# Down pieces taken in two parts between single gate and up pieces, and down weights laid two rows to a partition

## The chip, the core and the metric

The kernel runs on one core of a Trainium2 chip. The metric is device time in microseconds from start to end of one execution. Engines: PE (TensorE) multiplies matrices and loads their stationary operands (PEld in the profile); DVE (VectorE), ACT (ScalarE) and POOL (GpSimd) work on elements; SP (SyncE) issues transfers. Sixteen DMA engines move data between HBM and the on-chip memory SBUF; PE writes its results to PSUM.

## The reference

One encoder block on 528 tokens of width 1024: a mixer (attention beside a convolution), then a mixture of 16 experts in which every expert picks its 66 tokens. The part that this change touches is the experts':

```python
def one_group(hs):
    logits = jnp.einsum('ld,de->le', hs, w_router)
    aff = jax.nn.softmax(logits, axis=-1)
    g, idx = lax.top_k(aff.T, cap)                      # cap = 66
    xg = hs[idx]
    a = jnp.einsum('ecd,edf->ecf', xg, w_gate)          # d 1024, f 2048
    u = jnp.einsum('ecd,edf->ecf', xg, w_up)
    y = jnp.einsum('ecf,efd->ecd', jax.nn.silu(a) * u, w_down)
    y = y * g[..., None]
    out = jnp.zeros((L, D), y.dtype).at[idx.reshape(-1)].add(y.reshape(-1, D))
```

All weights are fp32, 24 MB for an expert.

## The kernel before

The mixer and the routing fill the first 355 us. Then a loop runs over the experts `e`. The weights come in pieces of 1 MB, 8 KB to each of 128 partitions, into a ring of 20 tiles called `raw`. A list `tasks`, written out by hand, sets the order of the pieces; `pump` issues a transfer for each free tile of the ring, in that order, and `nextw` hands PE the next piece and pumps again. A tile is free when PE has done its last matmul on it. SP issues nearly all transfers, so a transfer whose tile isn't free holds up those behind it.

An expert has 16 gate and up pieces (256 rows of the weights by 1024 columns, so two rows to a partition, row `p` and row `128 + p` of the piece) and 8 down pieces (256 rows by 1024 columns, laid out in the same way, two runs of 4 KB in a partition). In the loop over expert `e` PE works on gate and up pieces of expert `e` and on down pieces of expert `e - 1`.

- `prod` multiplies gate or up weights: the weights are the stationary operand, in halves of 64 columns, and the 66 chosen tokens `X` move past. Results go to PSUM as `G` or `U`, then through ACT (SiLU) and DVE (product) to `H`, in which partition `p` of slice `j` holds hidden unit `128 j + p`. A piece is 32 matmuls in the program; the chip runs each as two pairs of weight load and matmul, so a piece is 64 pairs in the trace.
- `down_piece` multiplies with down weights: 32 columns of `H` are the stationary operand and 512 columns of the weights move past. Four such matmuls run side by side on four column groups of PE (a set). A piece has three rounds `r` of four matmuls, which the chip runs as six sets, 24 pairs. Results add up in the PSUM tile `y`, three banks, which has one buffer.
- `to_tokens` scatters what an earlier expert gave (`yh`, `yl`) to the tokens by a matmul with a one-hot matrix: tile `T`, two matmuls; DVE adds it to `acc`.
- `down_rows`, at an expert's end, reads `y` with ACT and DVE (lines 980 to 987) and leaves `yh` and `yl`.

The order on PE is that of the program. With `i` counting the gate and up pieces of an expert, a token product and a whole down piece stand behind every odd `i`, so the pattern is two gate or up pieces, `T`, one down piece. I call it a group; there are eight in an expert. Expert 0 has gate and up pieces alone; the last expert's down pieces follow the loop, cut into 512 rows by 512 columns.

Of the kernel before, what the change touches and what calls it, by code (L numbers as in the profile page):

```python
# [19 lines left out]
P = 128  # L20
D = 1024
DC = D // P
# [32 lines left out]
def block_kernel(ctx: ExitStack, tc: tile.TileContext, x, meta, mix_g, w_in, conv_w, lq1, lk1, lq2,  # L55
                 lk2, sub_g, w_out, ffn_g, w_router, w_gate, w_up, w_down, fin_g, rope, out):
    nc = tc.nc
# [18 lines left out]
    def two(ap):  # L76
# [28 lines left out]
    rows = [(meta, NMETA, 0), (x[0, 0:128], 128, 16), (x[0, 128:256], 128, 144), (x[0, 256:384], 128, 272),  # L105
            (x[0, 384:496], 112, 400), (x[0, 496:512], NMETA, 512)]
# [121 lines left out]
    HS = (slice(0, HALF), slice(HALF, L))  # L228
# [353 lines left out]
    last = [Outs(0, c, None) for c in range(0, D, 256)]  # L582
# [132 lines left out]
    def moe_raw():  # L715
        i = moe_n[0] % NRAW
        moe_n[0] += 1
        for n, p in rings:
            if i < n:
                return p.tile([P, 2048], F32, name="raw", tag="raw")  # L720
            i -= n

    tasks = []
    def gate_up(e):
        return [w[0, e, k * 256:(k + 1) * 256, h * 1024:(h + 1) * 1024].rearrange("(c p) f -> p c f", p=P)
                for h in range(2) for w in (w_gate, w_up) for k in range(4)]

    def down(e):

        for d in range(8):  # L730
            rows, cols = slice(d * 256, (d + 1) * 256), slice(0, D)
            if e == NE - 1:
                rows, cols = slice(d % 4 * 512, (d % 4 + 1) * 512), slice(d // 4 * 512, (d // 4 + 1) * 512)
            yield w_down[0, e, rows, cols].rearrange("(c p) f -> p c f", p=P)


    for e in range(NE):
        dn = down(e - 1) if e else None
        for i, t in enumerate(gate_up(e)):
            tasks.append(t)  # L740
            if e and i % 2:
                tasks.append(next(dn))
    tasks.extend(down(NE - 1))
    queue = []

    def pump(n, eng=nc.sync):
        while len(queue) < n and tasks:
            t = moe_raw()
            a = tasks.pop(0)
            v = t.rearrange("p (c f) -> p c f", c=a.shape[1])  # L750
            if tasks:
                eng.dma_start(v, a)
            else:
                for k in range(2):
                    eng.dma_start(v[:, 2 * k:2 * k + 2], a[:, 2 * k:2 * k + 2])
            queue.append(t)

    pump(RING[0])


# [77 lines left out]
    nc.vector.tensor_tensor(af, af, r2[:, :, None].to_broadcast([P, NT, NE]), op=ALU.mult)  # L838
    nc.scalar.activation(af, af, AF.Exp)
    pump(NRAW - RING[3])  # L840
    late.close()

# [55 lines left out]
    def gather(e):  # L898
        xg = xgp.tile([CAP, D], F32, name="xg", tag="xg")
        nc.gpsimd.indirect_dma_start(out=xg, out_offset=None, in_=hn2_d,  # L900
                                     in_offset=bass.IndirectOffsetOnAxis(ap=idxT[:CAP, e:e + 1], axis=0))
        return xg
# [7 lines left out]
    last = const.tile([P, 2], F32, name="last")  # L910
# [16 lines left out]
    HS = [wk.tile([P, NF, CAP], F32, name=f"H{i}") for i in range(2)]  # L927
# [3 lines left out]
    def banks(tag, n):  # L931
        return ps2.tile([P, n, 512], F32, name=tag, tag=tag, bufs=1)

    def nextw():
        pump(NRAW)
        return queue.pop(0)

    def prod(out, w, c0, x, first, last):

        for q in range(2):  # L940
            nc.tensor.matmul(out[64 * q:64 * q + 64], w[:, c0 + 64 * q:c0 + 64 * q + 64], x, start=first, stop=last,  # L941
                             skip_group_check=True)

    def at(t, i):
        return t[:, i // 4, i % 4 * CAP:(i % 4 + 1) * CAP]

    def four(t, k):
        return t[:, k, :4 * CAP].rearrange("p (c n) -> p c n", n=CAP)

    def turn_x(X, xg, k):  # L950
        t = banks("T", 1)
        for i in range(4):
            nc.tensor.transpose(at(t, i), xg[:, (4 * k + i) * P:(4 * k + i + 1) * P], ident[:CAP, :CAP])  # L953
        nc.vector.tensor_tensor(X[:, 4 * k:4 * k + 4], four(t, 0),
                                gffn[:, 4 * k:4 * k + 4, None].to_broadcast([P, 4, CAP]), op=ALU.mult)

    def new_x():
        return wk.tile([P, DC, CAP], F32, name="X", tag="X", bufs=2)

    def down_piece(y, H, d):  # L960


        w = nextw()
        for r in range(3):
            ob, ci = ((0, 0), (0, 1), (1, 0))[r]
            o = ci * 1024 + ob * 512
            for g in range(3):
                nc.tensor.matmul(y[32 * g:32 * g + 32, ob], H[:, 2 * d + ci, GR[g]:GR[g] + 32], w[:, o:o + 512],  # L968
                                 start=d == 0 and r != 1, stop=d == 7 and r != 0, skip_group_check=True)
            nc.tensor.matmul(y[96:128, r], H[:, 2 * d + 1, GR[r]:GR[r] + 32], w[:, 1536:2048], start=d == 0, stop=d == 7,  # L970
                             skip_group_check=True)

    def down_rows(y, e):

        gate = at96[:96, NE + e:NE + e + 1]
        yh = wk.tile([96, D], FR, name="yh", tag="yh")
        yl = wk.tile([96, D], FR, name="yl", tag="yl")
        tmp = wk.tile([96, 512], F32, name="tmp", tag="tmp")
        a, b = slice(0, 512), slice(512, D)
        nc.scalar.activation(yh[:, a], y[:96, 0], AF.Copy, scale=gate)  # L980
        nc.vector.scalar_tensor_tensor(yl[:, a], y[:96, 0], gate, f32(yh[:, a]), op0=ALU.mult, op1=ALU.subtract)
        for g in range(3):
            gs = slice(32 * g, 32 * g + 32)
            nc.scalar.activation(tmp[gs], y[96:128, g], AF.Copy, scale=at96[gs, NE + e:NE + e + 1])
        nc.vector.scalar_tensor_tensor(tmp, y[:96, 1], gate, tmp, op0=ALU.mult, op1=ALU.add)
        nc.scalar.copy(yh[:, b], tmp)
        nc.vector.tensor_tensor(yl[:, b], tmp, f32(yh[:, b]), op=ALU.subtract)  # L987
        oh = wk.tile([96, 512], FR, name="oh", tag="oh")
        nc.gpsimd.tensor_scalar(oh, tok, at96[:96, e:e + 1], None, op0=ALU.is_equal)  # L989
        return oh, yh, yl  # L990

    def to_tokens(po, rows, d):

        oh, yh, yl = rows
        hf, t = divmod(d, 4)
        hfs = slice(hf * 512, (hf + 1) * 512)
        for n, b in enumerate((yh, yl)):
            nc.tensor.matmul(po, oh[:, t * P:(t + 1) * P], b[:, hfs], start=n == 0, stop=n == 1)  # L998
        nc.vector.tensor_tensor(acc[:, t, hfs], acc[:, t, hfs], po, op=ALU.add)  # L999
# [3 lines left out]
    X = new_x()  # L1003
# [3 lines left out]
    rows = None  # L1007
    for e in range(NE):
        H = HS[e % 2]
        y = banks("y", 3) if e else None  # L1010
        i = 0
        for h in range(2):
            for n in range(2):
                t = banks("GU"[n], 2)
                for k in range(4):
                    w = nextw()
                    for ci in range(2):
                        c = 2 * k + ci
                        for j in range(8):
                            prod(at(t, j), w, ci * 1024 + j * P, X[:, c], c == 0 and j % 4 == 0, c == DC - 1)  # L1020
                    if i % 2 and rows is not None:
                        to_tokens(banks("T", 1)[:, 0], rows, i // 2)
                    if i % 2 and e:
                        down_piece(y, HS[(e - 1) % 2], i // 2)
                    i += 1
                    if i in (10, 12) and e + 1 < NE:
                        if i == 10:
                            Xn = new_x()
                        turn_x(Xn, xg, i // 2 - 5)
                        if i == 12 and e + 2 < NE:  # L1030
                            xg = gather(e + 2)
                for k in range(2):
                    dst = H[:, 8 * h + 4 * k:8 * h + 4 * k + 4]
                    src = four(t, k)
                    if n == 0:
                        nc.scalar.activation(dst, src, AF.Silu)  # L1036
                    else:
                        nc.vector.tensor_tensor(dst, dst, src, op=ALU.mult)  # L1038
        if e:
            rows = down_rows(y, e - 1)  # L1040
        X = Xn
# [25 lines left out]
    for k in range(2):  # L1067
        t = moe_raw()
        o += [t[:, :D], t[:, D:]]
    t = moe_raw()  # L1070
# [7 lines left out]
    for i in range(8):  # L1078
        w = nextw()
        hf, d = divmod(i, 4)  # L1080
        for ci in range(4):
            f = 4 * d + ci
# [81 lines left out]
```

## Time and profile before

| what | value |
|---|---|
| runs | 1375.6, 1375.21 and 1371.81 us, median 1375.21 |
| profiled execution | 1375.47 us, of which the span from first to last instruction is 1373.7 us |
| PE busy | 1258.4 us, 92% of the span |
| weight loads busy (beside PE) | 929.4 us, 68% |
| DVE, ACT, POOL busy | 390.3, 232.0, 175.6 us |
| moved by DMA | 434.49 MB |
| mean granted TensorE clock | 0.968 |

An engine's busy share says how much of the span it had an instruction under way, and PE's matmuls overlap, so a busy PE isn't one at its peak. A share near 100% for two units at once doesn't tell which one sets the time. That is told by waits: who stood idle, and what ended it.

### The profile page before, as it was taken

The page shows a single profiled execution, that of the slowest core. Times are in us where ns is not written, and L with a number is a line of the kernel's source. Part 1 is how long each engine was busy: PE and PEld are TensorE (multiplying, and loading weights), DVE is VectorE, ACT ScalarE, POOL GpSimd, SP SyncE. Part 2 cuts the span into 40 slices and gives each one's busy share as a digit, 9 for nine tenths or more (in the row PEclk, how much of TensorE's full clock was granted, in tenths as well). Part 3 has the DMA queues.
Part 4 walks back from the last instruction along what each step waited for, and adds up shares of the span by engine and source line. Part 5 has one row for each costly group of instructions (what it writes and reads, how often), then busy time and mean ns, then how long its engine had stood idle before and what let it go on. Part 6 is the DMA issues. An engine that isn't in the chain of part 4 may idle for free.

```text
span 1373.7 us, 47053 instructions
## 1 busy us (share of the span) xinstructions
PE 1258.4 (92%) x22308; PEld 929.4 (68%) x22308; DVE 390.3 (28%) x668; ACT 232.0 (17%) x431; POOL 175.6 (13%) x139
## 2 busy tenths in 40 slices
PE   7888889995579999999999999999999999999996
PEld 6678889995566666666666666666666666665665
DVE  5876776554100111121111111111111111111114
ACT  4455444332000101010010101011010101010112
POOL 2734441231100000000000000000000000000002
PEclk9899889997799999999999999999999999999998
DMA  7311211295799999999999999999999999999994
GB/s 208 93 31 31 62 32 62 93 355 199 285 358 403 396 401 401 390 407 395 407 397 405 386 394 395 392 398 390 400 383 400 394 387 397 390 398 398 407 367 166
DMA packets 142881, 434.49 MB, mean 316 GB/s; under 512 B 13200, under 2 KB 37776, under 8 KB 142688
## 3 DMA queue, kind: packets, MB, share of 16 engines
q1 hardware_dynamic: 139936, 423.49, 80.6%
q0 software_dynamic: 2752, 8.00, 1.9%
q8 instruction: 174, 2.85, 0.9%
q14 instruction: 19, 0.16, 0.0%
HBM read 427.19 MB, written 4.26 MB: 314 GB/s over the span
## 4 chain that ended last, share of the span: by engine, by line
PE 76%; DMA 8%; DVE 7%; issue 4%; ACT 3%; POOL 1%; SPq 0%; DVEq 0%; ACTq 0%; POOLq 0%
PE y L968 21%; PE G L941 17%; PE U L941 17%; PE T L998 5%; PE pj L274 5%; DMA raw<-in_w_gate 4%; PE pj L304 3%; DMA raw<-in_w_up 3%; PE ys L941 1%; ACT qsw L365 1%; PE sc L430 1%; PE pj L344 1%; PE T L953 1%; ACT p L441 1%; DVE wl L234 1%
## 5 line engine op out<-in xcount | busy, mean ns | idle before, releaser
L968 PE MATMUL y<-raw,H 128*32 128x512 f32 x2160 | 336.9, 596 | 2.1 <-issue 2.1
L970 PE MATMUL y<-raw,H 128*32 128x512 f32 x720 | 331.9, 596 | 0.0
L941 PEld LDWEIGHTS U<-X,raw 128*64 128x64 f32 x8192 | 250.5, 138 | 65.1 <-issue 49.3
L941 PEld LDWEIGHTS G<-X,raw 128*64 128x64 f32 x8192 | 249.9, 139 | 59.7 <-issue 52.5
L941 PE MATMUL U<-X,raw 128*64 128x66 f32 x8192 | 262.9, 224 | 21.5 <-issue 16.7
L941 PE MATMUL G<-X,raw 128*64 128x66 f32 x8192 | 261.7, 224 | 19.3 <-issue 18.0
L999 DVE TENSOR_TENSOR acc<-acc,T 128x512 f32<-128x512 f32 x112 | 76.9, 687 | 600.0 <-PE T L998 600.0
L968 PEld LDWEIGHTS y<-raw,H 128*32 128x32 f32 x2160 | 79.8, 109 | 190.2 <-issue 175.2
L1036 ACT ACTIVATE H<-G 128x264 f32<-128x264 f32 x64 | 21.5, 388 | 592.0 <-PE G L941 592.0
L900 POOL DMA_INDIRECT xg<-hn_rows,idxT x16 | 16.3, 1017 | 694.8 <-PE T L953 675.2
L274 PE MATMUL pj<-xh,wl 128*128 128x264 f32 x320 | 70.0, 302 | 0.0
L970 PEld LDWEIGHTS y<-raw,H 128*32 128x32 f32 x720 | 69.1, 109 | 0.9 <-issue 0.6
L274 PE MATMUL pj<-xl,wh 128*128 128x264 f32 x320 | 68.6, 298 | 0.0
L274 PE MATMUL pj<-xh,wh 128*128 128x264 f32 x320 | 68.3, 297 | 0.0
L980 ACT ACTIVATE yh<-y,at 96x512 fp32r<-96x512 f32 x15 | 10.3, 684 | 282.2 <-PE y L970 282.2
L998 PE MATMUL T<-yh,oh 96*128 96x512 f32 x112 | 55.9, 499 | 1.6 <-issue 1.6
L274 PEld LDWEIGHTS pj<-xh,wl 128*128 128x128 f32 x320 | 53.9, 204 | 0.1
L274 PEld LDWEIGHTS pj<-xl,wh 128*128 128x128 f32 x320 | 53.3, 202 | 0.0
L274 PEld LDWEIGHTS pj<-xh,wh 128*128 128x128 f32 x320 | 53.3, 202 | 0.0
L989 POOL TENSOR_SCALAR oh<-tok,at 96x512 fp32r<-96x512 int16 x15 | 23.6, 1573 | 174.8 <-PE T L998 174.7
L998 PE MATMUL T<-yl,oh 96*128 96x512 f32 x112 | 44.4, 396 | 1.6 <-DVE yl L987 1.6
L1038 DVE TENSOR_TENSOR H<-H,U 128x264 f32<-128x264 f32 x64 | 24.4, 423 | 70.9 <-PE U L941 70.9
(225 smaller groups left out, 1181.5 us busy)
## 6 DMA issues: line engine op xcount, KB each, us to landing
raw<-in_w_up SPq DMA_DIRECT2D x128, 1024.0 KB, 11.1
raw<-in_w_gate SPq DMA_DIRECT2D x126, 1024.0 KB, 21.2
raw<-in_w_down SPq DMA_DIRECT2D x126, 1024.0 KB, 20.4
raw<-in_w_in SPq DMA_DIRECT2D x24, 512.0 KB, 4.2
raw<-in_w_out SPq DMA_DIRECT2D x8, 512.0 KB, 3.5
hn_rows<-raw SPq DMA_DIRECT2D x4, 512.0 KB
raw<-in_w_gate POOLq DMA_DIRECT2D x2, 1024.0 KB, 9.5
out<-raw SPq DMA_DIRECT2D x4, 512.0 KB, 4.6
```

The costliest lines, as they stand in the source:

```text
L234: nc.vector.tensor_tensor(lo, src, f32(hi), op=ALU.subtract)
L274: nc.tensor.matmul(o[:, hf * 512:hf * 512 + HALF], a[:, c], b[:, HS[hf]], start=c == 0 and n == 0, stop=c == DC - 1 and n == 2)
L304: nc.tensor.matmul(o[:, hf * 512:hf * 512 + HALF], a[:, k, i * P:(i + 1) * P], b[:, HS[hf]], start=k == 0 and n == 0, stop=k == 3 and n == 2)
L900: nc.gpsimd.indirect_dma_start(out=xg, out_offset=None, in_=hn2_d, in_offset=bass.IndirectOffsetOnAxis(ap=idxT[:CAP, e:e + 1], axis=0))
L941: nc.tensor.matmul(out[64 * q:64 * q + 64], w[:, c0 + 64 * q:c0 + 64 * q + 64], x, start=first, stop=last, skip_group_check=True)
L968: nc.tensor.matmul(y[32 * g:32 * g + 32, ob], H[:, 2 * d + ci, GR[g]:GR[g] + 32], w[:, o:o + 512], start=d == 0 and r != 1, stop=d == 7 an ...
L970: nc.tensor.matmul(y[96:128, r], H[:, 2 * d + 1, GR[r]:GR[r] + 32], w[:, 1536:2048], start=d == 0, stop=d == 7, skip_group_check=True)
L989: nc.gpsimd.tensor_scalar(oh, tok, at96[:96, e:e + 1], None, op0=ALU.is_equal)
L998: nc.tensor.matmul(po, oh[:, t * P:(t + 1) * P], b[:, hfs], start=n == 0, stop=n == 1)
L999: nc.vector.tensor_tensor(acc[:, t, hfs], acc[:, t, hfs], po, op=ALU.add)
L1036: nc.scalar.activation(dst, src, AF.Silu)
L1038: nc.vector.tensor_tensor(dst, dst, src, op=ALU.mult)
```

## The change

Three things change together. The order of the tasks: a down piece stands behind every gate or up piece with even `i` instead of odd, so a group's pieces come as gate, down, gate. The work on it: `down_piece` takes the piece and the rounds to run; round 0 runs behind even `i`, rounds 1 and 2 behind odd `i`, with the token product ahead of them. The layout: a down piece now puts rows `2p` and `2p + 1` of its 256 rows in partition `p`, so that a partition's 8 KB are one run in HBM. For this, `H` must hold its hidden units in the same order, and gate and up weights are read at every second column (`step=2`). The last expert's down pieces take rows in the same order; their runs stay 2 KB long.

```diff
             if e == NE - 1:
                 rows, cols = slice(d % 4 * 512, (d % 4 + 1) * 512), slice(d // 4 * 512, (d // 4 + 1) * 512)
-            yield w_down[0, e, rows, cols].rearrange("(c p) f -> p c f", p=P)
+                yield w_down[0, e, rows, cols].rearrange("(b p c) f -> p b c f", p=P, c=2)
+            else:
+                yield w_down[0, e, rows, cols].rearrange("(p c) f -> p c f", p=P)
...
-            if e and i % 2:
+            if e and i % 2 == 0:
                 tasks.append(next(dn))
...
-    def prod(out, w, c0, x, first, last):
+    def prod(out, w, c0, x, first, last, step=1):
 
         for q in range(2):
-            nc.tensor.matmul(out[64 * q:64 * q + 64], w[:, c0 + 64 * q:c0 + 64 * q + 64], x, start=first, stop=last,
+            c = c0 + 64 * q * step
+            nc.tensor.matmul(out[64 * q:64 * q + 64], w[:, c:c + 63 * step + 1:step], x, start=first, stop=last,
                              skip_group_check=True)
...
-    def down_piece(y, H, d):
-
-
-        w = nextw()
-        for r in range(3):
+    def down_piece(y, H, d, w, rounds):
+
+
+        for r in rounds:
...
-                            prod(at(t, j), w, ci * 1024 + j * P, X[:, c], c == 0 and j % 4 == 0, c == DC - 1)
+                            prod(at(t, j), w, ci * 1024 + j // 2 * 256 + j % 2, X[:, c], c == 0 and j % 4 == 0,
+                                 c == DC - 1, 2)
                     if i % 2 and rows is not None:
                         to_tokens(banks("T", 1)[:, 0], rows, i // 2)
-                    if i % 2 and e:
-                        down_piece(y, HS[(e - 1) % 2], i // 2)
+                    if e:
+                        if i % 2 == 0:
+                            wd = nextw()
+                        down_piece(y, HS[(e - 1) % 2], i // 2, wd, ((0,), (1, 2))[i % 2])
```

On PE, where one expert ends and the next begins, with the semaphores that an instruction waits for in brackets (DMAHW and DMASW tell of transfers, the others of engines). The names are those of the list above; the numbers behind `H` tell its two buffers apart. Before:

```order
L968 MATMUL y<-raw,H_3463 32x512 x3
L970 MATMUL y<-raw,H_3463 32x512
L941 MATMUL G<-X,raw 64x66 [waits DMAHW2_49,PE_49,Activation_49]
L941 MATMUL G<-X,raw 64x66 x31
L941 MATMUL G<-X,raw 64x66 [waits DMAHW3_49]
L941 MATMUL G<-X,raw 64x66 x31
L998 MATMUL T<-yh,oh 128x512 [waits DVE_49,Activation_49,Pool_49]
L998 MATMUL T<-yl,oh 128x512 [waits DVE_49]
L968 MATMUL y<-raw,H_3464 32x512 [waits DMAHW4_49,DVE_49,PE_49]
```

Two gate pieces and the token product stand between the last matmul on the old expert's `y` and the first on the new one's, which waits for DVE's last read of the old `y`, the instruction on line 985. The same place after the change:

```order
L970 MATMUL y<-raw,H_3463 32x512 x3
L972 MATMUL y<-raw,H_3463 32x512
L944 MATMUL G<-X,raw 64x66 [waits DMAHW2_49,PE_49,Activation_49]
L944 MATMUL G<-X,raw 64x66 x31
L970 MATMUL y<-raw,H_3464 32x512 [waits DMAHW3_49,DVE_49,PE_49]
L970 MATMUL y<-raw,H_3464 32x512 x2
L972 MATMUL y<-raw,H_3464 32x512
L944 MATMUL G<-X,raw 64x66 [waits DMAHW4_49]
L944 MATMUL G<-X,raw 64x66 x31
L1000 MATMUL T<-yh,oh 128x512 [waits Pool_49]
L1000 MATMUL T<-yl,oh 128x512
L970 MATMUL y<-raw,H_3464 32x512 x3
```

The first matmul on the new `y`, with the same wait, has moved ahead of the second gate piece and of the token product; one round stands there, and the other two stay behind the token product.

On SP, where the pieces of expert 1 and the first down pieces are issued, with each transfer's shape in SBUF. Before:

```order
L752 DMA raw<-in_w_up 128x2x1024
L752 DMA raw<-in_w_gate 128x2x1024 x2
L752 DMA raw<-in_w_down 128x2x1024
L752 DMA raw<-in_w_up 128x2x1024 x2
L752 DMA raw<-in_w_down 128x2x1024
```

And after the change:

```order
L753 DMA raw<-in_w_up 128x2x1024
L753 DMA raw<-in_w_gate 128x2x1024
L753 DMA raw<-in_w_down 128x2048
L753 DMA raw<-in_w_gate 128x2x1024
L753 DMA raw<-in_w_up 128x2x1024
L753 DMA raw<-in_w_down 128x2048
L753 DMA raw<-in_w_up 128x2x1024 x2
```

A down piece is now one run of 2048 elements in a partition where it was two of 1024, and it is issued one place earlier in its group.

## Rows read from the trace of the kernel before

**Rows 1.** Busy time by stage: stretch, length, engines busy (instructions), clock, DMA share, GB/s.
```profile
700.00:1150.00 450.00, 438.29 (x9040) 288.96 (x9034) 73.23 (x127) 36.20 (x68) 19.64 (x15) 1.00 1.02 394
1150.00:1331.00 181.00, 170.42 (x3513) 113.20 (x3508) 24.54 (x42) 10.73 (x22) 6.34 (x5) 0.99 1.01 393
```

**Rows 2.** PE's waits from 405 to 1150 us: total, times, longest.
```profile
PE U L941 <- issue: 8.9, 11, 1.4
PE G L941 <- issue: 8.8, 10, 1.7
PE y L968 <- issue: 2.1, 3, 0.9
PE T L998 <- issue: 1.6, 1, 1.6
```

**Rows 3.** PE's waits from 1150 to 1331 us.
```profile
PE U L941 <- DMA raw<-in_w_up: 4.6, 8, 2.0
PE G L941 <- issue: 3.2, 2, 1.9
...
PE G L941 <- DMA raw<-in_w_gate: 1.0, 3, 0.6
```

**Rows 4.** The page's first line, and the queue that brings instructions: packets, MB, share.
```profile
span 1373.7 us, 47053 instructions
...
q8 instruction: 174, 2.85, 0.9%
```

**Rows 5.** The chain that ended last, in expert 0 and early in expert 1: start, length.
```profile
371.74 3.95 PE U L941 x128
375.69 1.97 issue
...
378.46 3.15 PE G L941 x108
...
411.89 3.89 PE G L941 x128
415.78 0.56 PE y L968 x3
```

**Rows 6.** PE's instructions in order of time where expert 6 follows expert 5: start, length.
```profile
709.41 0.60 PE L968 MATMUL y<-raw,H 128*32 128x512 f32 x3
...
709.95 3.96 PE L941 MATMUL G<-X,raw 128*64 128x66 f32 x128
713.83 0.50 PE L998 MATMUL T<-yh,oh 96*128 96x512 f32 x1
...
714.56 0.63 PE L968 MATMUL y<-raw,H 128*32 128x512 f32 x3
...
714.99 0.63 PE L968 MATMUL y<-raw,H 128*32 128x512 f32 x3
...
717.28 3.96 PE L941 MATMUL G<-X,raw 128*64 128x66 f32 x128
```

**Rows 7.** ACT and DVE in the same stretch, reading the accumulator y.
```profile
710.11 0.68 ACT L980 ACTIVATE yh<-y,at 96x512 fp32r<-96x512 f32 x1 [18.92 <-PE y L970]
...
711.61 2.07 ACT L984 ACTIVATE tmp<-y,at 32x512 f32<-32x512 f32 x3 [0.81 <-DVE yl L981]
...
713.72 0.75 DVE L985 SCALAR_TENSOR_TENSOR tmp<-y,at,tmp 96x512 f32<-96x512 f32 x1 [2.14 <-ACT tmp L984]
```

**Rows 8.** The weights' queue from 600 to 640 us: packets, MB, share of 16 engines.
```profile
q1 hardware_dynamic: 4105, 15.83, 99.9%
```

**Rows 9.** The same queue from 1334 to 1344 us, runs of 2 KB.
```profile
q1 hardware_dynamic: 1813, 3.59, 99.3%
```

**Rows 10.** Weight loads on the page, of 64 and of 128 columns: busy, mean ns.
```profile
L941 PEld LDWEIGHTS G<-X,raw 128*64 128x64 f32 x8192 | 249.9, 139 | 59.7 <-issue 52.5
...
L274 PEld LDWEIGHTS pj<-xh,wl 128*128 128x128 f32 x320 | 53.9, 204 | 0.1
```

**Rows 11.** Busy time and granted clock around two gaps, columns as in rows 1.
```profile
1195.50:1198.20 2.70, 0.74 (x14) 0.34 (x12) 0.00 (x0) 0.00 (x0) 0.00 (x0) 1.00 1.00 316
1198.30:1201.70 3.40, 3.40 (x70) 3.40 (x66) 0.00 (x0) 0.00 (x0) 0.00 (x0) 0.50 1.03 406
...
1241.50:1245.00 3.50, 1.56 (x28) 0.99 (x28) 0.00 (x0) 0.00 (x0) 0.00 (x0) 1.00 1.01 403
```

More of the change, by code (lines that the diff above doesn't have):

```diff
@@ L749, in pump @@
             a = tasks.pop(0)
-            v = t.rearrange("p (c f) -> p c f", c=a.shape[1])
-            if tasks:
-                eng.dma_start(v, a)
+            if len(a.shape) == 3:
+                eng.dma_start(t.rearrange("p (c f) -> p c f", c=a.shape[1]), a)
             else:
+                v = t.rearrange("p (b c f) -> p b c f", b=2, c=2)
                 for k in range(2):
-                    eng.dma_start(v[:, 2 * k:2 * k + 2], a[:, 2 * k:2 * k + 2])
+                    eng.dma_start(v[:, k], a[:, k])
             queue.append(t)
```

## The prediction

> **What bounds the kernel now.** I began with the stages. From 355 us on the kernel is the expert loop; the loop over experts 1 to 15 runs from 407 to 1331 us. There DMA is busy at 1.01 to 1.02 of its 16 engines and PE at 94 to 97% [rows 1], so both look like the bound, and the stage table can't tell which. The list of PE's waits can. From 405 to 1150 us none of its rows names a DMA: PE never ran out of weights, since 20 pieces of 1 MB were loaded while routing ran and PE eats that stock slowly. Its idle time there is 8.9 + 8.8 + 2.1 + 1.6 us of "issue", a wait for nothing that the profile can name, in 25 gaps [rows 2]. Only after 1150 us does PE wait for weights, 4.6 + 1.0 us in 11 gaps, beside 3.2 us of issue [rows 3]. So at the end PE is level with the transfers, and before that PE sets its own pace. So what adds to PE's work beyond the few us of these last waits makes PE the bound from start to end.
>
> What is the issue wait? The queue of instructions carried 174 packets and 2.85 MB for 47053 instructions [rows 4], so 16.4 KB a packet and 61 B an instruction: one packet holds about 270 instructions, or some 135 pairs of weight load and matmul. In expert 0, where PE has gate and up pieces alone, it does 128 pairs in 3.95 us and then idles 1.97 us [rows 5]: 5.9 us for 256 instructions, however short their work. I read this as instructions arriving no faster than that. A later group (two gate or up pieces, a token product, a down piece) has 128 + 2 + 24 pairs, 308 instructions, in 7.3 us [rows 6], so 6.1 us for 256: level with the arrival, and idle wherever a packet's worth falls on the dense pieces.
>
> **The group, step by step.** Gate or up matmuls follow each other at 3.15 us / 108 = 29.2 ns [rows 5]. A burst of 128 pairs ends 3.88 us after its start (709.95 to 713.83), and 3.89 us where a down piece stands directly behind it (411.89 to 415.78) [rows 5, 6]. At 29.2 ns it would be 3.74, so leaving a burst costs 0.14. The down matmuls come in sets of four, 0.43 us apart (714.56, 714.99), but from the last set to the next gate matmul it is 0.54 us (709.41 to 709.95) [rows 6]; the way back costs 0.11 to 0.14.
>
> **Cost 1, more switches.** The changed group has two gate/up bursts of 64 pairs and two down bursts, of two and four sets, where there was one of each. It makes one more switch in each direction: 0.14 + 0.13 = 0.27 us. Eight groups in 15 experts: 120 x 0.27 = **+32 us** on PE. Bounds: nothing, if the loads are pulled ahead in short bursts, and 34 us.
>
> **Cost 2, a wait that had been covered.** The accumulator y has one buffer. After an expert's last down matmul ACT and DVE read it, in the chain 710.11, 711.61 (three of them), 713.72 + 0.75 = 714.47 us [rows 7]. The first down matmul of the next expert waits for DVE's last read. It starts at 714.56, right then, and costs nothing now: between the last y set (709.41) and it PE has 128 pairs and the token product, until 714.5 [rows 6]. The change puts 64 pairs ahead of it and nothing else: 64 x 29.2 ns + 0.14 = 2.0 us, so PE arrives at 709.95 + 2.0 = 711.95 and waits until 714.56, **2.6 us**. What stands behind it on PE, the second gate piece, the token product and all the rest, is late by as much; no other work of PE can pass it. Experts 1 to 14 each have a successor with such a wait: 14 x 2.6 = **+36 us**. The chain's length is not touched by the change. Bounds: 30 us (some of it falls where PE would have waited for instructions anyway) and 36.
>
> **Gain 1, more even instructions.** The idle time at issue sums to 24.6 us in 27 gaps [rows 2, 3]. A gap is counted from the end of the last matmul, 224 ns after its start, while the next would have come after 29 ns; so each costs 0.19 more, together 30 us. The changed group takes 7.3 + 0.27 = 7.57 us for 308 instructions, 6.3 us for 256, above the 5.9 of arrival, and no 128 pairs stand in one row any more. I take **-25 us** and leave 5, since the token product and the second down part are still 2.5 us with few instructions, which leaves the rest of such a packet's worth dense. Bounds: nothing and -30.
>
> **Gain 2, waits for weights.** With PE later, the 5.6 us in 11 gaps [rows 3], 7.7 us by the same account, fall away: **-8 us**.
>
> **The 8 KB runs.** While 4 KB runs move, 4105 packets with 15.83 MB took 0.999 of 16 engines for 40 us [rows 8], 165 ns for 4 KB; with 2 KB runs 3.59 MB took 0.993 for 10 us [rows 9], 91 ns for 2 KB. Two of these are 17 ns more than one of 4 KB. If halving the packets again saves that much, a down piece saves 8 x 17 ns = 0.13 us on each engine, and 120 of them 16 us of transfer. On the path it is worth **nothing**: PE is behind the transfers by then, and PE's work is the cover. Without that cover it would be worth the 8 us that PE waits for weights, which are counted already.
>
> **Weights read at every second column.** The gate and up loads now step over 8 bytes. No row of before shows a load with a step. Nothing is the lower bound. Above, 64 columns at a step span what 128 columns in a row do: 204 ns instead of 139 [rows 10]; loads go two side by side, so up to 33 ns on each of 16384 pairs, 541 us. Between ends so far apart I take nothing, being nearest to the row of the same 64 columns, and give the dear side to a rival. The Trainium skill (SBUF — State Buffer, section on door 1, the DMA port swizzle) says that reads keep full rate while they hit each 16-byte line twice, which a step of 8 bytes just does; by it this term is nothing, and no run here shows it yet.
>
> **The clock.** PE was idle for 2.0 of the 2.7 us from 1195.5 on, and then the granted clock was 0.50, the level of 1.2 GHz, from 1198.3 to 1201.7; in a stretch from 1241.5 that had 1.9 us idle it stayed 1.00 [rows 11]. 3.4 us at half speed lose 1.7. The 14 new waits are longer than these gaps; I take two or three drops, **+4 us**, between none and 24.
>
> **Sum.** 32 + 36 - 25 - 8 + 4 = +39 on the profiled execution's own 1375.5 us (span 1373.7 and 1.8 around it): **1414 us**. The median of the runs shown, 1375.2, is the same within 0.02%.
>
> **Rivals.** *The stream of transfers is the bound* (faster). DMA is over 100% busy through the whole loop [rows 1], and it is what PE meets at the end [rows 3]. Shorter by 16 us, it would let PE drop its 8 us of waits: 1368 us, no lower, since PE's own work stays. It decides if PE's additions stay under about 8 us, that is, if neither the switch nor the y wait is paid. Against it: no wait for a DMA before 1150 us. The Trainium skill has it so (SBUF — State Buffer, section on the bandwidth-pool intuition: HBM is almost always the end-to-end bottleneck, not SBUF); by that rule the result is this rival's, and the list of PE's waits disagrees up to 1150 us. *The switches are hidden* (no change): the y wait of 36 is paid, the 30 of issue and the 8 for weights are won: 1375.5 + 36 - 30 - 8 = 1373.5 us. For it: PE loads weights while it multiplies. Against it: the 0.11 to 0.14 us stand at every switch of the rows. *The stepped loads are dear* (slower still): each nanosecond on a pair costs 16 us, so two or more put it over 1442 us, up to 1916. *The changed runs do not become longer packets*: 4 KB packets stay; the time is that of the forecast, since that term is nothing.
>
> **Numbers.** Forecast 0.82, stepped loads dear 0.08, switches hidden 0.05, stream bound 0.05. The forecast's bounds: switches at half, gains at their most, no clock loss, 1375.5 + 16 + 30 - 30 - 8 = 1383; the first gain at half and ten clock drops, 1375.5 + 34 + 36 - 15 - 8 + 17 = 1440. Range 1383 to 1442; 0.18 is left out. Slower by over 0.3% (about what a measurement of this kernel tells from no change) 0.90, within 0.05, faster 0.05.
>
> **What would show it.** In the changed profile: PE or its sequencer waits about 2.6 us, 14 times, at y's first matmul behind DVE's last read of y; the group of 154 pairs takes about 7.5 us; issue idle falls below 10 us; no wait for weights after 1150 us; gate and up matmuls still 29 ns apart, weight loads still 139 ns; fewer and 8 KB packets on the weights' queue. I am wrong if y's first matmul waits under 1 us, if the group stays at 7.3 us, or if the loads take over 140 ns.

## The result

The changed kernel takes 1418.18 us (median of 5 runs, 1416.45 to 1420.96), the kernel before 1374.09 us beside it (5 runs). The ratio is 1.032 with an interval of [1.0307, 1.0333]: 44 us slower, 4 above the forecast. The profiled execution took 1416.58 us, its span is 1414.8 us, so 41 more than the span of before.

The stages of the changed kernel, columns as in [rows 1]:

```profile
700.00:1150.00 450.00, 431.75 (x8512) 275.83 (x8506) 68.23 (x117) 32.85 (x63) 18.08 (x14) 0.99 1.01 392
1150.00:1331.00 181.00, 172.04 (x3382) 109.57 (x3379) 27.67 (x47) 14.08 (x27) 7.36 (x6) 0.99 1.00 389
1331.00:1370.00 39.00, 39.00 (x800) 25.11 (x798) 4.12 (x7) 0.67 (x2) 1.56 (x1) 1.00 0.62 220
```

Up to 1331 us the table looks like that of before: DMA at 1.00 to 1.01, PE at 95 to 96%. By itself it would again not tell the bound. From 700 to 1150 us PE got through 8512 matmuls where it had got through 9040, and it was idle for 18.3 us instead of 11.7. The third line decides: DMA falls to 0.62 while PE is busy without a break, so the transfers were done and PE was not. By the trace's packets the last weights landed at 1356.05 us, 20 us before PE's first load of the last expert's down weights (1376.4); before, they landed at 1351.9, 18 us behind it (1333.9). The list of PE's waits over the whole loop says the same (total, times, longest):

```profile
PE y L970 <- issue: 34.6, 14, 2.7
PE U L944 <- issue: 2.7, 5, 0.8
PE G L944 <- issue: 1.2, 2, 1.0
PE T L1000 <- issue: 1.0, 1, 1.0
```

There is no row with a DMA any more, against 5.6 us in [rows 3]. The idle time at issue outside `y` is 4.9 us in 8 gaps; in [rows 2, 3] it was 24.6 us in 27. And one row is new: 34.6 us in 14 gaps ahead of the first matmul on `y`. The view names it "issue", as it does the late instructions, though it is something else. The instructions of line 970 by engine show what (duration least, median and most in ns, first and last start):

```profile
L970 PEldq EVENT_SEMAPHORE  x14: 2557/3166/3169, 461.5 to 1314.0; - x14
```

PE's queue of weight loads stood at a semaphore 14 times, 13 of them for 3.15 to 3.17 us and once for 2.56. PE's idle time is shorter than that because its last matmuls were still running. Where the loop over expert 4 follows that over expert 3, the timeline of PE reads (start, length):

```profile
589.47 0.59 PE L972 MATMUL y<-raw,H 128*32 128x512 f32 x1
590.00 2.15 PE L944 MATMUL G<-X,raw 128*64 128x66 f32 x64
594.61 0.63 PE L970 MATMUL y<-raw,H 128*32 128x512 f32 x3 [2.46 <-issue]
```

and that of DVE beside it:

```profile
593.76 0.75 DVE L987 SCALAR_TENSOR_TENSOR tmp<-y,at,tmp 96x512 f32<-96x512 f32 x1 [2.14 <-ACT tmp L986]
```

DVE's last read of the old `y` ends at 594.51 and PE goes on at 594.61. It is the chain of [rows 7], as long as it was, with only 64 pairs of weight load and matmul to cover it.

A group elsewhere in the loop, with nothing idle in it:

```profile
600.19 2.14 PE L944 MATMUL G<-X,raw 128*64 128x66 f32 x64
602.26 0.63 PE L970 MATMUL y<-raw,H 128*32 128x512 f32 x3
...
603.26 2.14 PE L944 MATMUL G<-X,raw 128*64 128x66 f32 x64
605.33 0.50 PE L1000 MATMUL T<-yh,oh 96*128 96x512 f32 x1
...
607.85 2.14 PE L944 MATMUL U<-X,raw 128*64 128x66 f32 x64
```

From 600.19 to 607.85 it takes 7.66 us. Before it was 3.885 for the 128 pairs, 0.66 for the token product and 2.71 for the down piece with the way back (each the shortest and the commonest time from start to start in the loop), 7.26 together. So a group is 0.40 us longer and 120 of them are 48 us. The prediction had 0.27.

The page's lines on transfers:

```profile
DMA packets 127632, 434.49 MB, mean 307 GB/s; under 512 B 13312, under 2 KB 37888, under 8 KB 112080
...
q1 hardware_dynamic: 124816, 423.49, 78.1%
```

All bytes are there, and 15552 of the packets are now 8 KB or more; 120 down pieces of 128 runs are 15360, and the instruction queue's 16 KB packets are most of the rest. A packet of 8 KB takes 313 ns on its engine (median over the trace), where two of 4 KB took 2 x 162.

### The profile page after: what moved, and what is told of

Same layout as the page of the kernel before. It is cut to its first block, busy times and chain, and to the rows that moved or that the text cites. A ratio compares the mean times of both kernels' runs of the same rounds, so it can differ in the third digit from the quotient of the medians.

```text
span 1414.8 us, 47033 instructions
## 1 busy us (share of the span) xinstructions
PE 1296.0 (92%) x22308; PEld 935.0 (66%) x22308; DVE 391.2 (28%) x668; ACT 232.1 (16%) x431; POOL 175.0 (12%) x139
## 4 chain that ended last, share of the span: by engine, by line
PE 84%; DVE 6%; issue 5%; ACT 3%; POOL 1%; DMA 1%; SPq 0%; DVEq 0%; ACTq 0%; POOLq 0%
PE y L970 24%; PE G L944 19%; PE U L944 19%; PE T L1000 5%; PE pj L274 4%; PE pj L304 3%; PE pj L344 1%; PE ys L944 1%; ACT qsw L365 1%; PE T L956 1%; PE sc L430 1%; ACT p L441 1%; DVE wl L234 1%; PE sc L794 1%; PE tr L461 1%
## 5 line engine op out<-in xcount | busy, mean ns | idle before, releaser
L970 PE MATMUL y<-raw,H 128*32 128x512 f32 x2160 | 359.5, 603 | 34.6 <-issue 34.6
L972 PE MATMUL y<-raw,H 128*32 128x512 f32 x720 | 356.2, 604 | 0.0
L944 PEld LDWEIGHTS G<-X,raw 128*64 128x64 f32 x8192 | 264.3, 141 | 97.9 <-issue 61.7
L944 PEld LDWEIGHTS U<-X,raw 128*64 128x64 f32 x8192 | 257.3, 138 | 101.6 <-issue 61.2
L944 PE MATMUL G<-X,raw 128*64 128x66 f32 x8192 | 282.3, 228 | 5.7 <-issue 5.7
L944 PE MATMUL U<-X,raw 128*64 128x66 f32 x8192 | 275.6, 225 | 10.3 <-issue 10.2
L970 PEld LDWEIGHTS y<-raw,H 128*32 128x32 f32 x2160 | 66.5, 108 | 156.5 <-issue 148.5
L972 PEld LDWEIGHTS y<-raw,H 128*32 128x32 f32 x720 | 59.5, 109 | 0.0
L274 PEld LDWEIGHTS pj<-xh,wh 128*128 128x128 f32 x320 | 52.2, 198 | 0.0
```

The source lines that it names most:

```text
L274: nc.tensor.matmul(o[:, hf * 512:hf * 512 + HALF], a[:, c], b[:, HS[hf]], start=c == 0 and n == 0, stop=c == DC - 1 and n == 2)
L944: nc.tensor.matmul(out[64 * q:64 * q + 64], w[:, c:c + 63 * step + 1:step], x, start=first, stop=last, skip_group_check=True)
```

## The experiments

Seven kernels, each timed over 5 rounds (5 to 12 executions) beside the kernel before (medians of 1375.4 us for the first four, 1374.7 us for the others). The theory that follows from the prediction: the wait for `y` and the switches make PE slower, the rest is near nothing. The rival: the loads at every second column are not free. All the edits are against the changed kernel, except where another one is named.

**The order alone.** Transfers, `H` and the reads of the weights are put back, the new order stays.

```diff
-                yield w_down[0, e, rows, cols].rearrange("(b p c) f -> p b c f", p=P, c=2)
-            else:
-                yield w_down[0, e, rows, cols].rearrange("(p c) f -> p c f", p=P)
+            yield w_down[0, e, rows, cols].rearrange("(c p) f -> p c f", p=P)
...
-                            prod(at(t, j), w, ci * 1024 + j // 2 * 256 + j % 2, X[:, c], c == 0 and j % 4 == 0,
-                                 c == DC - 1, 2)
+                            prod(at(t, j), w, ci * 1024 + j * P, X[:, c], c == 0 and j % 4 == 0, c == DC - 1)
```

> The new order on PE and of the transfers alone, with the old layout: no step in the weight loads, down pieces in runs of 4 KB. Theory 1 (the wait at y and the extra switches are the whole loss, the step costs nothing): like the changed kernel, 1415 to 1421 us, a group still 7.66 us. Theory 2 (the step costs PE about 0.05 us per piece of 64 pairs, 13 us in 256 pieces, and the switches only the 0.27 us a group that was forecast): about 1405 us, a group 7.53 us. In both, 14 waits of 2.6 us at y.

Measured: 1408.89 us, ratio 1.0241 [1.0221, 1.026]. That is 9.3 us less than the whole change, between the two theories and nearer to the second. The wait for `y` is the same:

```profile
PE y L967 <- issue: 35.5, 14, 2.7
...
```

The list begins with that row. In the timeline a group reads

```profile
604.01 2.09 PE L941 MATMUL G<-X,raw 128*64 128x66 f32 x64
...
607.03 2.09 PE L941 MATMUL G<-X,raw 128*64 128x66 f32 x64
609.04 0.50 PE L997 MATMUL T<-yh,oh 96*128 96x512 f32 x1
...
611.56 2.09 PE L941 MATMUL U<-X,raw 128*64 128x66 f32 x64
```

and so takes 7.55 us. Each burst of 64 pairs ends 2.018 us after its start, against 2.072 in the changed kernel (commonest times from start to start). So of the 0.40 us that a group has grown, 0.29 are switches (35 us in 120 groups) and 0.108 are the step (13 us). That the total differs by 9.3 and not by 13 fits the sum of lost time under "Gains 1 and 2" below, by which this kernel loses 3 us more in the loop than the changed one, in somewhat longer waits for `y` and more late instructions.

**The layout alone.** The old order with 8 KB runs and the step.

```diff
-            if e and i % 2 == 0:
+            if e and i % 2:
                 tasks.append(next(dn))
...
-                    if e:
-                        if i % 2 == 0:
-                            wd = nextw()
-                        down_piece(y, HS[(e - 1) % 2], i // 2, wd, ((0,), (1, 2))[i % 2])
+                    if i % 2 and e:
+                        down_piece(y, HS[(e - 1) % 2], i // 2, nextw(), range(3))
```

> The new layout alone (8 KB runs, stepped weight loads), with the old order. Theory 1 (the step costs nothing): PE's 8 us of waits for weights go, about 1366 us. Theory 2 (step 0.05 us per piece): PE gains 13 us of work, loses the 8 us of waits and a few us of issue idle: 1374 to 1380 us, a group of 128 pairs, T and 24 pairs at 7.36 instead of 7.26 us. No wait at y in either.

Measured: 1365.46 us, ratio 0.9934 [0.9917, 0.9951]: faster than both kernels, by 9 to 10 us and by 53. PE's waits in the loop:

```profile
PE G L944 <- issue: 8.4, 11, 1.6
PE U L944 <- issue: 7.4, 11, 1.2
PE T L1000 <- issue: 1.7, 1, 1.7
PE y L970 <- issue: 0.8, 2, 0.5
...
```

The waits for weights are gone; what is left out are three rows of the tail. A burst of 128 pairs with nothing idle in it takes 3.99 us, 0.11 more than before. Here it goes from 715.55 to 719.55:

```profile
715.55 4.06 PE L944 MATMUL G<-X,raw 128*64 128x66 f32 x128
719.55 0.50 PE L1000 MATMUL T<-yh,oh 96*128 96x512 f32 x1
```

That is not to be seen in the total, which is theory 1's though its reason, a step without a price, is not: idle time at issue is 18.3 us in 25 gaps where it was 24.6 in 27.

**8 KB runs without the step.** The kernel above, with weights read column by column. `H` then holds its hidden units in another order than the down rows, so another product is computed; the work is the same.

```diff
-                            prod(at(t, j), w, ci * 1024 + j // 2 * 256 + j % 2, X[:, c], c == 0 and j % 4 == 0,
-                                 c == DC - 1, 2)
+                            prod(at(t, j), w, ci * 1024 + j * P, X[:, c], c == 0 and j % 4 == 0,
+                                 c == DC - 1)
```

> As the layout alone, but gate and up columns are read without the step, so that the hidden units and the rows of the down weights no longer belong together: the product is another one, the work the same. It shows what the 8 KB runs alone are worth. Longer packets shorten the stream of transfers by 16 us: then PE's waits for weights go and the time is 1366 to 1368 us. Rival (packets of 8 KB move no faster): 1374 us, with 5 us of waits for weights after 1150 us as before.

Measured: 1366.19 us, ratio 0.9936 [0.9918, 0.9953]; a burst of 128 pairs takes 3.885 us again. Idle time at issue is 25.5 us in 30 gaps:

```profile
PE U L944 <- issue: 10.8, 13, 1.4
PE G L944 <- issue: 10.1, 12, 1.7
PE y L970 <- issue: 2.7, 4, 1.3
PE T L1000 <- issue: 1.9, 1, 1.9
...
```

So the longer runs alone are worth 9 us in the old order, about the 8 that the prediction gave them without PE's cover. With and without the step the time is the same within the intervals: in the old order the step's 13 us of PE work lie where PE would have waited for instructions. The sum of lost time under "Gains 1 and 2" has it: 33 us with the step, 45 without.

**The wait for y covered.** Each expert's first down piece is worked on whole behind the second gate piece, so that 128 pairs and the token product lie between the old `y` and the new one again. The order of the transfers is untouched.

```diff
-                        down_piece(y, HS[(e - 1) % 2], i // 2, wd, ((0,), (1, 2))[i % 2])
+                        down_piece(y, HS[(e - 1) % 2], i // 2, wd,
+                                   ((0,), (1, 2))[i % 2] if i > 1 else ((), (0, 1, 2))[i])
```

> The changed kernel, but each expert's first down piece runs whole behind the second gate piece and the token product, as before the change; the other seven pieces stay split. Theory 1 (wait at y): the 14 waits fall to nothing, 36 us, with 4 or 5 drops of the clock that followed them, 7 us: 1373 to 1384 us. Rival (the loss is spread over all groups, from switches or from stepped loads, and the wait at y only stands where PE would have been idle anyway): 1405 to 1418 us.

Measured: 1377.5 us, ratio 1.0022 [1.0011, 1.0034]. This one edit takes back 41 of the 44 us, as theory 1 said. The wait is gone from the list of PE's waits:

```profile
PE G L944 <- issue: 4.4, 5, 1.1
PE U L944 <- issue: 1.8, 4, 0.6
...
```

**The same without the step.** The edit of the kernel without the step on top (another product, as there).

> The changed kernel with each expert's first down piece whole behind its second gate piece (the wait for y covered) and with gate and up weights read without a step (hidden units and down rows then don't belong together, so another product is computed). With the step this kernel took 1377.5 us, with 6 us of issue idle in the loop and no wait for weights. Theory A (the step costs 0.85 ns on each of 15 times 1024 pairs behind the table of 16 experts, 13 us, and in the new order PE has no idle time to hide it): 1362 to 1368 us, the group at 7.55 us instead of 7.66. Theory B (the step costs nothing on the total in this order either, as it did in the old one): 1376 to 1379 us.

Measured: 1370.5 us, ratio 0.997 [0.9959, 0.9981]: 7.0 us less. The step's work in the loop is 13 us. From 405 to 1370 us the idle time at issue rises from 6.2 us in 9 gaps to 9.8 in 15:

```profile
PE G L944 <- issue: 6.3, 8, 1.3
PE U L944 <- issue: 2.5, 6, 0.8
PE ys L944 <- issue: 1.0, 1, 1.0
...
```

With 0.19 us for each gap, as in the prediction, that is 4.7 us of the 13; 8 are left, and 7.0 were measured. Neither theory had it: one said 9 to 15, the other nothing. In the new order the step is paid by half. (The sum of lost time, which also takes in delays too short to be a gap, is 5 us higher without the step.)

**The order alone, wait covered.** The edit that covers the wait, on the kernel with the order alone.

> The new order alone, in the old layout (runs of 4 KB, no step), with each expert's first down piece whole behind its second gate piece, so that the wait for y is covered. It leaves of the change the switches (120 times 0.29 us, 35 us) and the more even instructions (25 us of issue idle saved). Theory A (the step is worth 13 us when PE is the bound, and the runs of 8 KB nothing then): 1364 to 1370 us, a little more if PE comes level with the transfers again: in that case waits for weights of up to 9 us show after 1150 us, and 1370 to 1376 us. Theory B (the step costs nothing, switches alone make the rest of the loss): 1376 to 1380 us, like the same kernel with the changed layout, 1377.5 us.

Measured: 1376.24 us, ratio 1.0012 [1.0003, 1.0021]. The time lies in theory B's range and 0.24 us above theory A's, so by itself it tells little between them. The list of PE's waits tells more. Theory A named the condition under which it comes near this time, and waits for weights are back, 4.1 us where it allowed up to 9.

```profile
PE G L941 <- issue: 5.5, 6, 1.3
PE U L941 <- issue: 3.1, 7, 0.6
PE U L941 <- DMA raw<-in_w_up: 2.4, 2, 1.5
PE G L941 <- DMA raw<-in_w_gate: 1.7, 2, 1.0
...
```

Beside the kernel without the step above, which differs by the 8 KB runs alone, it is 5.7 us slower. So runs of 8 KB give some 6 us and the step takes 7, once `y` doesn't hold PE up. The runs count here because PE has come level with the transfers again; theory B was wrong to put the step at nothing.

**Every fourth column.** The kernel with the layout alone, at step 4 (another product, as above).

```diff
-                            prod(at(t, j), w, ci * 1024 + j // 2 * 256 + j % 2, X[:, c], c == 0 and j % 4 == 0,
-                                 c == DC - 1, 2)
+                            prod(at(t, j), w, ci * 1024 + j // 4 * 512 + j % 4, X[:, c], c == 0 and j % 4 == 0,
+                                 c == DC - 1, 4)
```

> The kernel with the old order, runs of 8 KB, and gate and up weights read at every fourth column instead of every second (hidden units then stand in another order than the down rows, so another product is computed). With every second column a burst of 128 pairs took 3.996 us against 3.885 of unstepped loads, and the time was 1365.46 us against 1366.19. Theory A (a step costs by what lies between the columns; from step one to two 0.85 ns on a pair): step four adds two more such parts, 2.6 ns over no step, a burst of 128 pairs takes 4.2 us, PE's work grows by 28 us over the kernel with step two, of which the issue idle there (18 us) hides a part: 1372 to 1393 us. Theory B (the step's price is paid once, however long the step): 4.0 us a burst and 1364 to 1368 us. Theory C (a step that no longer takes two neighbours of 16 bytes halves the rate of the load, the reading that the Trainium skill, page SBUF — State Buffer, section on door 1, suggests): a load of 64 columns takes as long as one of 128 or longer, a burst of 128 pairs 6 us or more, the total over 1600 us.

Measured: 1805.6 us, ratio 1.3132 [1.3115, 1.3149]. A burst of 128 pairs in the timeline (start, length), with the token product behind it:

```profile
603.41 7.89 PE L944 MATMUL G<-X,raw 128*64 128x66 f32 x128
611.24 0.50 PE L1000 MATMUL T<-yh,oh 96*128 96x512 f32 x1
```

and the weight loads on the page (busy, mean ns of one, then idle time ahead of them):

```profile
L944 PEld LDWEIGHTS G<-X,raw 128*64 128x64 f32 x8192 | 496.5, 216 | 38.9 <-issue 37.7
```

A burst takes 7.83 us instead of 3.99, and a load 216 ns, a little more than one of 128 columns in a row in [rows 10]. Theories A and B fall as they were priced, theory C stands. From start to start a pair takes 60 ns, 30 more than at step 2, which would be 490 us on 16384 pairs. The 440 measured are less since in this kernel nothing in the loop is idle: the list of PE's waits from 405 to 1370 us has no row at all, and expert 0 has lost its gaps too. By the sum of lost time below, the kernel at step 2 loses 33 us in the loop and this one nothing; expert 0 makes the other 17. No step of three or eight was run, so a price that climbs steeply with the step, without an edge at 16 bytes, isn't ruled out by steps 1, 2 and 4.

## Why the prediction came out right, and where its terms were off

**The bound.** Right. PE set the pace from start to end; the transfers ended ahead of it. The rival by which the stream is the bound needed PE's additions to stay under 8 us. They were some ten times that. The sentence of the Trainium skill behind it (SBUF — State Buffer, section on the bandwidth-pool intuition), that HBM is almost always the end-to-end bottleneck, not SBUF, is not borne out by the changed kernel: PE waited for no weights there, nor in the kernel with the order alone, whose runs are still 4 KB. The last part of the old order agrees with it; there the 8 KB runs took away the waits for weights, and alone they gave 9 us.

**Cost 2, the wait for y.** Right: 14 waits, 36 us forecast, 34.6 us of idle time in the list; from start to start 2.55 us each, 35.6 us. The edit that covers it brought 40.7 us back. That is more than the wait alone: the edit also leaves the down piece of 15 groups whole (15 x 0.29 = 4.3) and ends the drops of the clock that followed the waits (8.5, below). From the 48 that these three make, 6 go to late instructions, which lose 14 us in that kernel's loop and 8 in the changed one's, by the sum below; that leaves 42.

**Cost 1, more switches.** Right: 32 us forecast, 0.29 us a group and 35 us measured in the kernel with the order alone. The rival by which they are hidden falls: no burst in the loop of that kernel ended under 2.017 us, where 64 pairs at 29.2 ns are 1.87.

**Weights read at every second column.** This is the term that was mis-sized: "Between ends so far apart I take nothing". It costs 0.054 us on 64 pairs, 0.85 ns on a pair, 13 us in the groups of the loop. It is what makes the group 7.66 us where 7.57 were forecast. The prediction said that each nanosecond on a pair costs 16 us, so at 0.85 the forecast would have been 1428; the gains below took most of that back. (The dear rival's upper end, 1916, is 541 on the time before; on the forecast it would be 1955.) The Trainium skill (SBUF — State Buffer, section on door 1, the DMA port swizzle) says that reads keep full rate as long as they touch each 16-byte line twice. The runs agree with where it puts the edge: at step 2, two columns to 16 bytes, a burst of 128 pairs went from 3.885 to 3.99 us; at step 4, one column to 16 bytes, to 7.83. They don't agree that the free side is quite free: 3% a pair, which by that rule is nothing. So the dear rival's price exists, at a step that this change does not reach; the prediction's "being nearest to the row of the same 64 columns" was no reason that could have told step 2 from step 4. Its sign of being wrong, loads over 140 ns, was met by the letter and for another reason: on the page of the changed kernel the `G` loads average 141 ns, but so they do in the kernel with the order alone, which has no step, and outside the half-clock stretches below both average 138 or less.

**Gains 1 and 2.** Larger than forecast, 42 us instead of 33. Summed from the starts of PE's instructions in the loop, each burst's time over its shortest, before lost 51.7 us. 1.7 of these belong to the half clock of [rows 11], 50 to late instructions and weights. The prediction took the listed gaps, with 0.19 us added to each, 30 + 8 = 38. The list leaves out delays too short to be a gap. After loses 52.2 us by the same sum: 35.6 at `y`, 8.5 to the clock, 8 to the rest. So 42 of the 50 were won. The same sum gives 55 us for the order alone, 33 for the layout alone, 45 for the 8 KB runs without the step, 14 for the wait covered, 19 for that without the step, 25 for the order alone with the wait covered and nothing for step 4. That "issue" means late instructions, which the prediction only inferred from averages, can be read from the trace of before: each of the 27 gaps ends 1.31 to 1.62 us after a 16 KB packet of the instruction queue has landed, and in the changed kernel so do all 8 gaps outside `y`.

**The clock.** The granted clock was 0.50, the level of 1.2 GHz, five times in the loop, each time for about 3.4 us right behind a wait for `y`. The first and the last of them, and the stretch ahead of the first:

```profile
657.00:661.00 4.00, 1.52 (x25) 0.58 (x23) 1.44 (x2) 2.35 (x4) 0.00 (x0) 0.99 1.02 410
661.00:664.40 3.40, 3.40 (x61) 3.27 (x58) 0.00 (x0) 0.00 (x0) 0.00 (x0) 0.50 0.97 394
...
1251.60:1254.80 3.20, 3.20 (x48) 2.20 (x42) 0.69 (x1) 0.02 (x1) 0.00 (x0) 0.50 1.03 422
```

Five at 1.7 us are 8.5, against 1.7 before: 6.8 more, where 4 were forecast. In the kernel whose wait is covered no stretch at half clock stands in the loop over experts 1 to 15. The kernel with the order alone has five too. Nine of the 14 waits, as long as the others, were followed by none; what sets these apart stays open.

**The 8 KB runs.** Right that they become longer packets, that they cost nothing, and that they would be worth 8 us without PE's cover (9 and 5.7 measured). That they are worth nothing on this path follows from the kernel with the order alone, in which PE waits for no weights though the runs are 4 KB; it was not timed by itself.

**The sum.** In the loop 35 + 13 + 35.6 + 6.8 - 42 = +48; the first gate matmul starts 2.1 us earlier, expert 0 and the first gate pieces of expert 1 lose 2.7 less, and the tail is 1.4 shorter, so +42 by the terms and +41 in the span. Before, expert 0 ended in a gap with a half clock behind it:

```profile
399.00:403.00 4.00, 0.45 (x14) 0.46 (x16) 0.00 (x0) 0.00 (x0) 0.00 (x0) 1.00 1.02 376
403.00:406.40 3.40, 3.40 (x69) 3.40 (x67) 0.77 (x2) 0.00 (x0) 0.00 (x0) 0.50 0.99 369
```

The profile after has no half clock there. That it comes or stays away there differs among the kernels above and was not traced to its cause. So the total was met within 4 us partly by luck: a cost taken at nothing (13 us) and gains taken too small (9 us) nearly balance.

## What to carry to other kernels

Before work is moved ahead, find the buffer that it writes and ask which drain it now runs into: here one round of four matmuls pulled ahead by half a group met a drain of 4.4 us that 128 pairs and a token product had hidden exactly, and covering it again took back 41 of the 44 us. Take apart a change that bundles several edits: this one held a gain of 9 us (the longer runs) beside 53 us of loss, and its better half, the layout alone at 1365.46 us, beats both kernels. A strided read of a stationary operand should be priced with a larger step as well as with its own, since the price here was 3% at a step of two and some 100% at a step of four.

## What the runs showed of the hardware

- A load of 64 fp32 columns: pairs of load and matmul follow each other at 29.2 ns with neighbouring columns, at 30.0 with every second and at 60 with every fourth; the load itself shows 139, 139 and 216 ns. At step 2 the load's own duration does not show the price, only the spacing of the pairs does.
- A cost on PE's work can vanish in one order and not in another: the same 13 us of stepped loads moved the total by less than 1 us where PE waits for instructions anyway (18 to 26 us of issue idle) and by 7.0 us where it waits little (6 to 10 us).
- PE's waits at "issue" end when instructions arrive: in the kernel before, each of 27 gaps ended 1.31 to 1.62 us after a packet of 16 KB had landed on the instruction queue, and these packets came 6.3 us apart (median).
- A packet of 8 KB took 313 ns, one of 4 KB 162 ns and one of 2 KB 84 ns: a whole piece of 8 KB runs saves some 11 ns on each pair of packets joined, where the prediction estimated 17.
